# Twelve gate projections as six seven-product pairs in a stage of their own, with input sums made during attention

## The chip, the cores and the metric

The kernel runs on one core of one Trainium2 chip. The metric is device time in microseconds (us) from the start to the end of one launch. Engines are named as the profile names them: PE is the matrix engine (PEld its weight loads), DVE the vector engine, ACT the scalar engine, POOL the GpSimd engine, and SP the engine whose queue issues most DMAs. PSUM is the matrix engine's accumulation memory, of which a bank holds a 128x512 float32 tile. Each engine works through its instructions in the order in which they were written.

## The reference

One decoder layer on x of 1024 tokens by 1024 features, all in float32:

```python
mod = silu(c) @ w_ada + b_ada                     # six rows of 1024: shift_m .. gate_f
u = x * (1 + scale_m) + shift_m
qa, ka, va, qb, kb, vb, ga, gb = split(u @ w_in)  # ga, gb: 1024 columns each
ya = window_attention(qa, ka, va) @ w_branch_a
yb = dilated_attention(qb, kb, vb) @ w_branch_b   # three patterns, merged
y = (sigmoid(ga) * ya + sigmoid(gb) * yb) @ w_o
x = layer_norm(ALPHA * x + (1 + gate_m) * y)
u = x * (1 + scale_f) + shift_f
h = u @ w_gate_up; y = (silu(h_g) * h_u) @ w_down
out = layer_norm(ALPHA * x + (1 + gate_f) * y)
```

The change concerns the sixteen 128-column chunks of `ga` and `gb` (numbers 0 to 15 here), the gates.

## The kernel before

Every float32 product is made of three fp32r matmuls. Both operands are split into a high part (an ACT copy to fp32r) and a low part (a DVE subtraction), and `mac` adds high by high, high by low and low by high (lines 138 to 140). A matmul takes 128 rows of weights by 512 tokens. The tokens stand in two halves t = 0 and 1, the 1024 features in eight blocks k.

`Weights` (object `ws`) is the list of weight pieces of 128x512 in the order of their use. `ws.step` takes the next one: the DMA into `w_raw` (three buffers, sent ahead on SP's queue), the ACT copy to `w_hi` and the DVE subtraction to `w_lo` (lines 78 and 79, four buffers). Where a piece has a scale (the pieces of w_o and w_down), POOL multiplies the raw piece first (line 62).

The stages that matter here, with their times in the profile:

- Attention, to 785 us. Projections of u, scores, exponentials and weighting are interleaved. Gates 3, 6, 4 and 5 are made here too, and their sigmoids stored in `ga_d` in memory. The attention outputs go to memory (`oa_d`, `ob_d`).
- Gates and branches, 785 to 1053.6 us. There are 24 branch steps (`steps`, b = 0, 1, 2 by eight chunks dc), each of 24 matmuls of an attention output (`o_hl`, split by `o_part`) with a chunk of branch weights, and `merge` puts the result into `zt`: for b = 0 an ACT copy, for b = 1 a DVE addition and a POOL multiplication by the gate, for b = 2 a DVE multiplication by the gate into `gy` and a POOL addition (line 968). A list `order`, worked out ahead, puts one gate projection (`make_gate`, 48 matmuls of u with two weight pieces) in front of each branch step that needs one. Twelve gates are made here. `split_merged` then splits the merged chunks into `m` (lines 118 and 119).
- Between these, `ada_steps` is a generator that makes the rows 2 to 5 of `mod`: for each row m, eight DMAs of `a_raw`, one DVE multiplication and seven DVE multiply-adds into `acc` (lines 915 and 917), and at the end of the row a short PE matmul of `acc` with ones (line 926 or 933). One `next(ada)` does one of about ten steps of a row, and 41 of them finish all four. They are called from `make_gate` (twice in each of ten gates) and after each branch step.
- The product with w_o, from 1053.6 us, which opens with eight PSUM banks, one for each block of 128 tokens.
- The feed-forward stage, 1144 to 1569 us. It treats two output chunks with the two token halves and the two feature halves as a 2x2 block product and needs seven half products in place of eight (`PRODUCTS`). Each half product is 12 matmuls. Sums of weight pieces are made by POOL (`g_sums`, four additions for a pair), and sums of the input (`t1` to `t4`) by DVE.

Of the kernel before, what the change touches and what calls it, by code (L numbers as in the profile page):

```python
# [10 lines left out]
F32 = mybir.dt.float32  # L11
# [85 lines left out]

@with_exitstack
def decoder_layer(ctx: ExitStack, tc: tile.TileContext, I, out, dbg=None):
# [28 lines left out]
    def wide(name, pool, halves=(0, 1)):  # L128

        ts = {(s, t, k): pool.tile([P, 4, TH], F32R, name=f"{name}{s}{t}{k}", tag="big")  # L130
              for t in halves for k in range(2) for s in range(2)}
        return lambda s, t, k: ts[s, t, k // 4][:, k % 4]

    u = wide("u", bigu)
# [22 lines left out]
    gate_of = {8 + dc: 46 + dc for dc in range(KC)}  # L157
    gate_of.update({16 + dc: 54 + dc for dc in range(KC)})
    branch_w = [I["w_branch_a"][0], I["w_branch_a"][1], I["w_branch_b"]]
    made_early = [8 + dc for dc in (early_gate_dc, lead_gate_dc, *tail_gates)]  # L160
    bridge = 10
    order = []
    for i in range(len(steps)):
        g = 8 if i == 0 else i + 1
        if g in gate_of and i != 7:
            order.append(("g", g))
        if i == 0:
            order.append(("b", bridge))
        order.append(("w", i))
    for kind, i in order:  # L170
        if kind == "b" or (kind == "g" and i not in (*made_early, bridge)):
            add_chunk(I["w_in"][gate_of[i]], 2, 4)
        elif kind == "w":
            b, dc = steps[i]
            add_chunk(branch_w[b][dc], 1, 4)
# [41 lines left out]
    ga_d = dram.tile([KC, P, T], F32, name="ga_d")  # L217
# [9 lines left out]
    with tc.tile_pool(name="pro", bufs=2) as pro:  # L227
# [55 lines left out]
        def ada_sum(j, ss=(0, 1)):  # L283
# [4 lines left out]
            if j not in mod_t:  # L288
                mod_t[j] = pro.tile([P, 2], F32, name="mod", bufs=3)
# [385 lines left out]
    def send_sums(p):  # L675
# [5 lines left out]
        side(p)[0].dma_start(wa_d[p].rearrange("h (b q) -> (h b) q", q=P), sr[:16])  # L681

    def fetch_bcast(key, src):
        last = key == A_PAIRS - 1 or key in [(B_PAIRS - 1, g) for g in range(3)]
        wb = att.tile([P, T], F32, name="vt" if last else "wb", bufs=1)
        for h in range(2):
            side(key)[0].dma_start(wb[h * 64:(h + 1) * 64], src[h:h + 1].to_broadcast([64, T]))
        sums[key] = wb

    def side(p):  # L690

        return (nc.gpsimd, nc.gpsimd) if p == A_PAIRS - 1 else (nc.sync, nc.vector)

    def scale_a(p):
        o = outs.pop(p)
        side(p)[1].tensor_tensor(o, o, sums.pop(p), op=OP.mult)
        side(p)[0].dma_start(oa_d[p], o)
# [819 lines left out]
```

## Time and profile before

| what | value |
|---|---|
| runs | 1816.66, 1817.24, 1817.37 us, median 1817.24 |
| the profiled execution | 1817.83 us, of which the span from first to last instruction is 1816.1 us |
| busy time: PE, DVE, ACT, POOL | 1802.8, 1071.2, 763.0, 572.6 us |
| stage of gates and branches | 785.1 to 1053.6 us, 268.5 us |

The span leaves out 1.7 us that lie around it. A row of the timeline gives the start in us, the busy time in us, engine, line, operation, the names and shapes of what it writes and reads, how many were merged into the row, and in brackets the idle time ahead of it and what ended that. Matmuls overlap, so the busy time of one is longer than the distance between two.

### The profile page before, as it was taken

What the parts mean: (1) busy time and instruction counts of PE and PEld (TensorE: products, weight loads), DVE (VectorE), ACT (ScalarE), POOL (GpSimd) and SP (SyncE); (2) the same over time, 40 slices, a digit from 0 to 9 for tenths busy, and PEclk for the clock granted to TensorE, in tenths of its full rate; (3) what the DMA queues carried; (4) which work ended last, traced back from release to release, by engine and by line L of the source; (5) the groups of instructions that cost most, each with busy time, mean ns of one, the idle gap of its engine ahead of it and who ended that gap; (6) DMA issues with size and microseconds to landing.
All of it is one profiled execution on the core that took longest, in us unless ns stands there. A gap on an engine that the chain in (4) does not pass through costs nothing.

```text
span 1816.1 us, 24384 instructions
## 1 busy us (share of the span) xinstructions
PE 1802.8 (99%) x8978; PEld 1484.6 (82%) x8978; DVE 1071.2 (59%) x1979; ACT 763.0 (42%) x1650; POOL 572.6 (32%) x372
## 2 busy tenths in 40 slices
PE   9999999999999999999999999999999999999998
PEld 7888888888888888788888888788888888888886
DVE  7754466556556766533654466766565444764557
ACT  6644444444444777643121133743333333421122
POOL 0232233233333232110421253156574333532223
PEclk9999999999999999999999999999999999999999
DMA  9322232232231232254633223042222222442222
GB/s 360 93 74 69 54 89 83 60 88 82 60 83 65 68 99 70 82 181 168 232 122 134 104 99 128 12 151 82 84 79 82 93 82 88 151 141 79 93 76 93
DMA packets 78008, 187.60 MB, mean 103 GB/s; under 512 B 14081, under 2 KB 15681, under 8 KB 77889
## 3 DMA queue, kind: packets, MB, share of 16 engines
q1 hardware_dynamic: 77408, 184.92, 31.1%
q8 instruction: 71, 1.16, 0.3%
q0 software_dynamic: 336, 1.06, 0.2%
q14 instruction: 49, 0.39, 0.1%
q10 hardware_dynamic: 144, 0.07, 0.0%
HBM read 147.37 MB, written 25.00 MB: 95 GB/s over the span
## 4 chain that ended last, share of the span: by engine, by line
PE 89%; DVE 5%; ACT 2%; issue 1%; DMA 1%; POOL 1%; SPq 0%; DVEq 0%
PE pf L1222 22%; PE pj L138 8%; PE pj L140 8%; PE pj L139 8%; PE p L138 6%; PE p L140 6%; PE p L139 6%; PE pf L140 5%; PE pf L138 5%; PE pf L139 5%; PE s L583 4%; PE po L644 3%; PE pt L621 3%; DVE qs L525 1%; DMA wa<-in_w_ada_m 1%
## 5 line engine op out<-in xcount | busy, mean ns | idle before, releaser
L138 PE MATMUL pj<-u,w_hi 128*128 128x512 f32 x736 | 302.8, 411 | 0.0
L140 PE MATMUL pj<-u,w_lo 128*128 128x512 f32 x736 | 288.5, 392 | 0.0
L139 PE MATMUL pj<-u,w_hi 128*128 128x512 f32 x736 | 288.1, 391 | 0.0
L510 POOL TENSOR_TENSOR rb<-rb,sin_t 128x512 f32<-128x512 f32 x64 | 85.7, 1339 | 517.2 <-DVE rb L508 452.3
L119 DVE TENSOR_TENSOR w_lo<-r,w_hi 128x512 fp32r<-128x512 f32 x106 | 114.4, 1082 | 132.9 <-ACT w_hi L118 132.9
L79 DVE TENSOR_TENSOR w_lo<-w_raw,w_hi 128x512 fp32r<-128x512 f32 x148 | 132.9, 902 | 90.5 <-ACT w_hi L78 88.7
L138 PEld LDWEIGHTS pj<-u,w_hi 128*128 128x128 f32 x736 | 138.7, 188 | 31.4 <-issue 6.7
L140 PEld LDWEIGHTS pj<-u,w_lo 128*128 128x128 f32 x736 | 138.3, 188 | 30.7
L599 ACT ACTIVATE probs<-probs,st 128x128 f32<-128x128 f32 (+1 forms) x320 | 145.6, 461 | 32.6 <-DVE st L588 32.3
L139 PEld LDWEIGHTS pj<-u,w_hi 128*128 128x128 f32 x736 | 138.9, 189 | 22.2
L140 PE MATMUL pf<-wd,h 128*128 128x512 f32 x352 | 137.1, 389 | 0.0
L139 PE MATMUL pf<-wd,h 128*128 128x512 f32 x352 | 137.1, 389 | 0.0
L138 PE MATMUL pf<-wd,h 128*128 128x512 f32 x352 | 137.1, 389 | 0.0
L62 POOL TENSOR_TENSOR w_raw<-w_raw,gate 128x512 f32<-128x512 f32 x60 | 84.9, 1432 | 151.0 <-DMA w_raw<-in_w_down 124.7
L1430 DVE SCALAR_TENSOR_TENSOR zt<-zt,pf 128x512 f32<-128x512 f32 x112 | 75.3, 685 | 80.1 <-PE pf L140 80.1
L511 POOL TENSOR_TENSOR r<-ra,rb 128x512 f32<-128x512 f32 x63 | 115.4, 1832 | 4.9
L78 ACT ACTIVATE w_hi<-w_raw 128x512 fp32r<-128x512 f32 x148 | 90.7, 623 | 40.8 <-PE p L139 28.1
L623 ACT ACTIVATE ptsb<-pt 128x512 f32<-128x512 f32 (+1 forms) x128 | 63.5, 549 | 101.5 <-PE pt L621 101.3
L583 PE MATMUL s<-kh,qs 128*128 128x256 f32 (+1 forms) x320 | 79.7, 283 | 2.1 <-DVE st L588 1.5
L524 ACT ACTIVATE qs<-r 64x1024 fp32r<-64x1024 f32 x38 | 40.2, 1058 | 98.7 <-POOL r L511 98.2
L525 DVE TENSOR_TENSOR qs<-r,qs 64x1024 fp32r<-64x1024 f32 x38 | 46.3, 1219 | 57.3 <-ACT qs L524 56.6
L583 PE MATMUL s<-kl,qs 128*128 128x256 f32 (+1 forms) x320 | 80.0, 279 | 0.0
(323 smaller groups left out, 4279.7 us busy)
## 6 DMA issues: line engine op xcount, KB each, us to landing
w_raw<-in_w_in SPq DMA_DIRECT2D x116, 256.0 KB
r<-in_w_gate_up SPq DMA_DIRECT2D x44, 512.0 KB
a_raw<-in_w_ada SPq DMA_DIRECT2D x32, 512.0 KB
w_raw<-in_w_down SPq DMA_DIRECT2D x44, 256.0 KB
h_raw<-h_d SPq DMA_DIRECT2D x22, 512.0 KB
h_d<-g SPq DMA_DIRECT2D x39, 256.0 KB
wa<-in_w_ada_m SPq DMA_DIRECT2D x16, 512.0 KB
kh<-kh SPq DMA_DIRECT2D x26, 256.0 KB
```

Source lines behind the costliest of these rows:

```text
L62: self.nc.gpsimd.tensor_tensor(self.raws[i], self.raws[i], scale(), op=OP.mult)
L78: self.nc.scalar.activation(hi, raw, AF.Copy)
L79: self.nc.vector.tensor_tensor(lo, raw, hi, op=OP.subtract)
L119: nc.vector.tensor_tensor(lo, src, hi, op=OP.subtract)
L138: nc.tensor.matmul(ps, w[0], m[0], start=first, stop=False)
L139: nc.tensor.matmul(ps, w[0], m[1], start=False, stop=False)
L140: nc.tensor.matmul(ps, w[1], m[0], start=False, stop=last)
L510: eng.tensor_tensor(b, b, sin_t[:, s], op=OP.mult)
L511: eng.tensor_tensor(residue_half(res, r, t), by_residue(a, r), by_residue(b, r), op=OP.add)
L583: nc.tensor.matmul(pss[h][:, i, lo:], box["q"][h][:, b * P:(b + 1) * P], ks[h][:, (b - 1 + lo) * P:(b + 1) * P], start=i == 0 and n == 0, ...
L599: nc.scalar.activation(pr, pr, AF.Exp, scale=-1.0, bias=st[:, 0, h, b:b + 1], accum_out=st[:, 1, h, b:b + 1])
L1222: nc.tensor.matmul(ps, w[:, c], m[:, k], start=first and k == 0 and n == 0, stop=k == 3 and n == 2, skip_group_check=True)
```

## The change

The seven-product form is taken over for the twelve gates that were made among the branches. They become six pairs (`gate_pairs`), made in a stage of their own between attention and the branches. The functions of the feed-forward stage for weight sums and splits move into a class `Pairs`, which both stages use. POOL makes the weight sums of the gates as well.

The sums of the input are made while attention runs (`input_sums`, eight times): two DMAs bring parts of x back into the buffer `cst`, two ACT instructions make u of them, four DVE subtractions the sums, and one DMA stores them in `t_d`. The new stage loads them again, 16 tiles `xs` of 128x512, and splits each (`next_sums`).

The first eight half products (two for each of the first four pairs) need the parts of u alone and open the stage. In them pieces of `ws` serve as weights. All sixteen gates now go through `ga_d`, and each branch step of b = 1 and 2 loads its gate (`fetch_gate`). The branch steps follow each other without gates between them. The steps of `ada_steps` are called 14 times in the new stage and 24 times after the branch steps, and the rest is run off behind the last `split_merged`, as before in the code.

The scaling of the last attention pair moves from POOL to DVE, into `o_part`; `split_merged` takes one chunk after each of the last six branch steps, and the chunks 6 and 7 at the end.

```diff
+class Pairs:
...
+    def add(self, p, step, own=None):
+        r1, r2 = self.raws[p]
+        tt = self.nc.gpsimd.tensor_tensor
+        if step == 0:
+            self.sums[p] = own or [self.pool.tile([P, TH], F32, name=n, bufs=1) for n in ("s1", "s2")]
+            tt(self.sums[p][0], r2[:, H0], r2[:, H1], op=OP.add)
+        elif step == 1:
+            tt(self.sums[p][1], self.sums[p][0], r1[:, H0], op=OP.subtract)
+        elif step == 2:
+            tt(r2[:, H0], r1[:, H0], r2[:, H0], op=OP.subtract)
+        else:
+            tt(r1[:, H1], r1[:, H1], self.sums[p][1], op=OP.subtract)
...
+    gate_pairs = ((0, 1), (2, 7), (8, 9), (10, 11), (12, 13), (14, 15))
+    EARLY_PAIRS = 4
+    for x, _ in gate_pairs[:EARLY_PAIRS]:
+        add_chunk(I["w_in"][46 + x], 2, 4)
+    for b, dc in steps:
+        add_chunk(branch_w[b][dc], 1, 4)
...
+        if n % 3 and n < 12:
+            input_sums(*divmod(2 * (n // 3) + n % 3 - 1, 2), i)
...
+        if i == 1:
+            for h in range(2):
+                part, mod = buf[:, h * TH:(h + 1) * TH], mods[k + 4 * h]
+                nc.scalar.activation(part, part, AF.Identity, bias=mod[:, 0:1], scale=mod[:, 1:2])
+        elif i == 2:
+            nc.vector.tensor_tensor(r11, r12, r11, op=OP.subtract)
+            nc.vector.tensor_tensor(r12, r22, r12, op=OP.subtract)
+            nc.vector.tensor_tensor(r22, r22, r11, op=OP.subtract)
+            nc.vector.tensor_tensor(r21, r21, r22, op=OP.subtract)
...
+    for n in range(2 * EARLY_PAIRS):
+        p, i = divmod(n, 2)
+        acc.setdefault(p, []).append(ps_2.tile([P, TH], F32, name="p2"))
+        product(gw, acc[p][i], i, True)
+        while len(gw.ready) < min(3, 2 * EARLY_PAIRS - 1 - n):
+            piece()
+        prepare(n + 4 - 2 * EARLY_PAIRS)
+        next_sums(2)
+        after()
...
+            prepare(n + 3)
...
+            product(gw, ps[bank], i, i in (0, 1, 3))
...
+            if i in (2, 3, 4) and not last:
+                gw.add(p + 1, i - 2)
+            if i == 4 and p + 2 < len(gate_pairs):
+                gw.load(p + 2)
...
+            elif p and i in (1, 2, 4, 6) or (p == 1 and i == 3):
                 next(ada, None)
...
-    for kind, i in order:
-        if kind == "b":
-            make_gate(i, kept=True, then=lambda: parts.append(o_part(0)))
-            continue
-        if kind == "g":
...
+    for i, (b, dc) in enumerate(steps):
...
         for t in range(2):
             merge(b, dc, t, ps[t], gts.get(i))
         next(ada, None)
-        if i == 22:
-            split_merged(range(3, 6))
+        fetch_gate(i + 1)
+        if i == 2 * KC + 1:
+            mg, _ = wide("m", bigu)
+        if i >= 2 * KC + 2:
+            split_merged((i - 2 * KC - 2,))
     split_merged(range(6, 8))
     for _ in ada:
         pass
```

Two places show how the order on the engines moves. The first is the passage from the last branch step to the product with w_o. On PE, the matmuls of `acc` with ones that finish row 5 stood inside a gate projection before (`u` with `w_hi` and `w_lo`):

```order
L140 MATMUL p_9296<-u_82,w_lo 128x512
L926 MATMUL p_9324<-acc,ones 128x512
L926 MATMUL p_9327<-acc,ones 128x512
L138 MATMUL p_9296<-u_82,w_hi 128x512
L139 MATMUL p_9296<-u_83,w_hi 128x512
```

Now they stand between the last matmul of the last branch step (`o_hl`) and the first of the product with w_o (`m`):

```order
L193 MATMUL p_9700<-o_hl,w_lo 128x512
L998 MATMUL p_9761<-acc,ones 128x512
L998 MATMUL p_9764<-acc,ones 128x512
L191 MATMUL p_9770<-w_hi,m_9452 128x512
L192 MATMUL p_9770<-w_lo,m_9452 128x512
```

So the matmuls of row 5 now stand at the seam of the two stages; before they stood 80 rows of PE ahead of it.

On DVE, before, the last branch step was followed by its two gate multiplications (`gy`) and the four splits of chunks 6 and 7:

```order
L79 TENSOR_TENSOR w_lo<-w_raw,w_hi 128x512 x2
L967 TENSOR_TENSOR gy<-p_9444,gt 128x512
L967 TENSOR_TENSOR gy<-p_9445,gt 128x512
L119 TENSOR_TENSOR m_9374<-zt,m_9373 128x512
L119 TENSOR_TENSOR m_9378<-zt,m_9377 128x512
L79 TENSOR_TENSOR w_lo<-w_raw,w_hi 128x512 x5
```

Now the last two multiply-adds of row 5 (`acc`) are there too. The first follows the gate multiplications, ahead of the two splits of chunk 5:

```order
L1196 TENSOR_TENSOR gy<-p_9699,gt 128x512
L1196 TENSOR_TENSOR gy<-p_9700,gt 128x512
L989 SCALAR_TENSOR_TENSOR acc<-a_raw,c_act,acc 128x1024
L170 TENSOR_TENSOR m_9455<-zt,m_9454 128x512
L170 TENSOR_TENSOR m_9459<-zt,m_9458 128x512
```

Four more splits, of chunks 6 and 7, follow these two. The last two of them and what comes behind (`gate` is row 5, finished from what the PE matmuls of `acc` give):

```order
L170 TENSOR_TENSOR m_9455<-zt,m_9454 128x512
L170 TENSOR_TENSOR m_9459<-zt,m_9458 128x512
L989 SCALAR_TENSOR_TENSOR acc<-a_raw,c_act,acc 128x1024
L999 TENSOR_TENSOR gate_9759<-p_9761,gate_9759 128x512
L999 TENSOR_TENSOR gate_9759<-p_9764,gate_9759 128x512
```

The last multiply-add stands behind all of these splits, and the PE matmuls of `acc` read what it writes.

The second place is the start of the new stage, on ACT. Before, the weights of gate 0 were followed by the attention outputs and by the tanh of a gate:

```order
L759 ACTIVATE r<-pj 128x512
L78 ACTIVATE w_hi<-w_raw 128x512 x2
L118 ACTIVATE o_hl<-o_raw 128x1024 x3
L759 ACTIVATE gt<-p_7599 128x512
L759 ACTIVATE gt<-p_7600 128x512
L78 ACTIVATE w_hi<-w_raw 128x512
```

Now weight pieces alternate with the loaded sums `xs`, two by two:

```order
L825 DMA ga_d<-r 128x1024
L78 ACTIVATE w_hi<-w_raw 128x512 x2
L1019 ACTIVATE t2h<-xs 128x512 x2
L78 ACTIVATE w_hi<-w_raw 128x512
L1019 ACTIVATE t2h<-xs 128x512 x2
L78 ACTIVATE w_hi<-w_raw 128x512
L1019 ACTIVATE t1h<-xs 128x512 x2
```

Each `w_hi` of an opening product, from the third piece made here on, stands behind copies that wait for a load from memory.

More of the change, by code (lines that the diff above doesn't have):

```diff
@@ L939, in decoder_layer @@
     gts = {}
[L941 to L956 removed]
+    B = {}
@@ new lines, in next_sums, with piece @@
+    def next_sums(n):
+        for _ in range(n):
+            if t_todo:
+                name, k = t_todo.pop(0)
+                split_to(name, k, t_raw.pop((name, k)))
+                if len(t_todo) > 3:
+                    load_sum(*t_todo[3])
+    def piece():
+        ws.step()
+        gw.ready.append(ws.done[ws.used][:2])
+        ws.used += 1
+    gw.load(0)
+    for x in t_todo[:4]:
+        load_sum(*x)
+    gw.load(1)
+    for step in range(4):
+        gw.add(0, step)
+    acc, gated = {}, {}
@@ L958, in merge, with mrg, fetch_gate @@
+    after()
+    after()
+    gp_ctx.close()
+    zp = ctx.enter_context(tc.tile_pool(name="zp", bufs=2, side="right", reuse_waits="tile"))
+    merged = [zp.tile([P, 4, T], F32, name="zt", tag="zt") for _ in range(2)]
+    def mrg(dc, t):
+        return merged[dc // 4][:, dc % 4, t * TH:(t + 1) * TH]
+    def fetch_gate(i):
+        if KC <= i < len(steps):
+            gts[i] = mix.tile([P, T], F32, name="gt", bufs=2)
+            nc.sync.dma_start(gts[i], ga_d[i - KC])
     def merge(b, dc, t, ps, g):
@@ L1010, in decoder_layer @@
             ws.step()
+        if (b == 0 and 2 <= dc < 6) or (b == 1 and dc in (3, 5)):
+            following.append(o_part(low))
+        if b == 1 and dc == KC - 1:
+            following += [o_part(low) for _ in range(2)]
+        if dc == KC - 1:
+            parts, following = following, []
         for t in range(2):
@@ L1209, in g_split @@
-    def g_split(p, i):
-        hi, lo = [wpool.tile([P, 512], F32R, name=s, tag=s, bufs=4) for s in ("w_hi", "w_lo")]
-        split(hi, lo, g_source(p, i))
-        ready.append((hi, lo))
-    def product(ps, i, first, between=None):
-        hi, lo = ready.pop(0)
-        b = B[PRODUCTS[i]]
-        for k in range(4):
-            if k == 3 and between:
-                between()
-            c = slice(k * P, (k + 1) * P)
-            for n, (w, m) in enumerate(((hi, b[0]), (hi, b[1]), (lo, b[0]))):
-                nc.tensor.matmul(ps, w[:, c], m[:, k], start=first and k == 0 and n == 0, stop=k == 3 and n == 2,
-                                 skip_group_check=True)
@@ L1291, in decoder_layer @@
         if n:
-            g_split(*opening[n + 3])
+            gu.split(*opening[n + 3])
         if n in (2, 4, 6):
```

342 lines of the change are left out of this document (204 added, 138 removed).

## The prediction

> **What bounds the kernel now.** I read the page's busy times first, then who makes PE wait, then windows over the stages, then the timeline at the seam that the change rebuilds. The first row gives busy time, share of the span and count; the second is the largest wait of PE for another engine (total us, times, longest).
>
> ```profile
> PE 1802.8 (99%) x8978; PEld 1484.6 (82%) x8978; DVE 1071.2 (59%) x1979; ACT 763.0 (42%) x1650; POOL 572.6 (32%) x372
> PE s L583 <- DVE st L588: 1.5, 6, 0.3
> ```
>
> PE is busy for 1802.8 of 1816.1 us, and its largest wait adds up to 1.5 us. So the kernel lasts as long as PE has work, and fewer matmuls shorten it, as long as nobody makes PE wait. The next rows are windows (length, then busy us and count of PE, PEld, DVE, ACT, POOL, then granted clock, DMA share, GB/s): attention, the stage of gates and branches, the opening of the seven-product form in the feed-forward stage, one pair of that form later on, and the load at the start of the kernel.
>
> ```profile
> 58.40:785.00 726.60, 724.54 (x4180) 594.67 (x4178) 435.01 (x1132) 386.24 (x1038) 207.81 (x130) 1.00 0.27 77
> 785.10:1053.60 268.50, 268.50 (x1194) 221.56 (x1195) 138.17 (x167) 69.49 (x116) 56.50 (x38) 1.00 0.45 156
> 1163.40:1182.40 19.00, 18.08 (x77) 14.02 (x76) 18.56 (x29) 16.42 (x29) 1.60 (x1) 1.00 0.07 23
> 1278.00:1297.00 19.00, 19.00 (x86) 15.74 (x85) 11.14 (x11) 7.26 (x14) 12.27 (x7) 1.00 0.23 83
> 15.00:20.00 5.00, 3.86 (x16) 2.58 (x15) 3.93 (x7) 3.86 (x5) 0.00 (x0) 1.00 1.03 413
> ```
>
> Gates and branches leave PE no gap at all, with DVE half idle. The form that is now copied holds PE at 19.00 of 19 us in its steady state, but lost 0.92 us in its opening, where DVE was busy for 18.56 of 19 us.
>
> **The matmuls taken away.** Twelve gates of 48 matmuls are 576; six pairs of 84 are 504. So 72 of 128x512 fall away. Their price is not the 0.39 us of a row but the distance between two:
>
> ```profile
> 1042.67 0.39 PE L138 MATMUL p<-o_hl,w_hi 128*128 128x512 f32 x1
> ...
> 1053.33 0.39 PE L140 MATMUL p<-o_hl,w_lo 128*128 128x512 f32 x1
> 1053.56 0.39 PE L138 MATMUL p<-w_hi,m 128*128 128x512 f32 x1
> ```
>
> The first of these rows opens the last but one branch step and the third follows the last, so 48 matmuls take 10.89 us, 0.227 us each. **Term 1: 72 x 0.227 = -16.3 us.** By the 0.39 us it would be -28, which overlapping work does not give.
>
> **The input sums in attention.** Eight times two ACT copies with scale, four DVE subtractions of 128x256, two loads and one store. By the split of a 128x512 tile (0.69 us alone, below), half of it for a subtraction: 32 x 0.35 = 11 us of DVE; 16 x 0.62 us = 10 us of ACT. In attention DVE idles for 292 us and ACT for 340. Behind these on their engines stand the reductions and exponentials of scores, for which PE waits. The loads stand on SP behind weight pieces, and `cst` is shared with the softmax merge, whose DMAs are a unit (some 40 us) away. **Term 2: 0**, with an upper end of 2 us, if each of the eight makes PE wait once for the 0.3 us of the wait row, and a lower end of 0, as none is removed. The last pair's scaling (POOL before, DVE in `o_part` now) is under the cover of branch matmuls both times.
>
> **The opening and the pairs.** Eight products of 12 x 0.227 = 2.72 us, 21.8 us. DVE has in them 9 low parts of weights and 16 of `xs`, 25 x 0.62 = 15.5 us, and three additions and sigmoid steps, 4 us: 19.5 of 21.8. The copied form lost 0.92 us at such a load. The loads run in two sets of two buffers: 1.2 us to issue, about 3 us to land (the row below is a 512 KB store from POOL's queue; none of SP's is timed), two ACT copies 1.24 and a split 0.62 make 6.1 us, so a set per 3.0 us against 2.72 of PE.
>
> ```profile
> oa_d<-o POOLq DMA_DIRECT2D x1, 512.0 KB, 3.0
> ```
>
> Then the first four pairs have five products left, 13.6 us, with five POOL instructions and three or four `ada` steps each. DVE's own part is 5 x 0.62 + 4 x 1.28 + 0.69 + 3 x 0.4 = 10.1 us, and POOL holds it up (below) by up to 5 x 1.05 = 5.3 us: 15.4 against 13.6 at the worst, with two products (5.4 us) of lead. **Term 3: +1.5 us**, near the measured 0.92, with ends 0 (the steady pair's row) and 8 (four pairs by 1.8 us and 1 us of opening). Gates stored and loaded add some 17 MB to a stage of 252 us, 67 GB/s on top of 156; the start moved 413 GB/s, so I cost that at nothing.
>
> **The seam, where I expect the gain to go.** Behind the last branch step PE now has the matmul of `acc` that finishes row 5, ahead of all of w_o. It needs the last multiply-add, which DVE has behind two gate multiplications, another multiply-add and six splits. `next(ada)` is called 14 + 24 = 38 times where 41 are needed; before there were 20 + 24 = 44, and row 5 was done 80 PE rows earlier. This seam before, on DVE and POOL:
>
> ```profile
> 1044.03 3.70 DVE L119 TENSOR_TENSOR m<-zt,m 128x512 fp32r<-128x512 f32 x6
> 1047.64 0.69 DVE L79 TENSOR_TENSOR w_lo<-w_raw,w_hi 128x512 fp32r<-128x512 f32 x1
> 1054.96 1.28 DVE L79 TENSOR_TENSOR w_lo<-w_raw,w_hi 128x512 fp32r<-128x512 f32 x2
> 1056.16 1.28 DVE L967 TENSOR_TENSOR gy<-p,gt 128x512 f32<-128x512 f32 x2
> 1057.36 6.57 DVE L119 TENSOR_TENSOR m<-zt,m 128x512 fp32r<-128x512 f32 x4
> 1056.99 2.99 POOL L968 TENSOR_TENSOR zt<-zt,gy 128x512 f32<-128x512 f32 x2 [4.91 <-DVE gy L967]
> 1059.95 5.13 POOL L62 TENSOR_TENSOR w_raw<-w_raw,gate 128x512 f32<-128x512 f32 x3
> L917 DVE SCALAR_TENSOR_TENSOR acc<-a_raw,c_act,acc x28: 1272/1279/2234, 819.8 to 1021.8; 128x1024 f32<-128x1024 f32 x28
> ```
>
> Six splits alone took 3.70 us, 0.62 each. Four of them beside POOL's additions and scalings took 6.57 in place of 2.5: each of the four POOL instructions that ran meanwhile cost DVE about 1.05 us. The two take turns on what they read, which a single pair shows too: the POOL addition grew from 1.3 to 2.26 us behind a multiply-add, and the split after it from 0.69 to 1.78.
>
> ```profile
> 998.26 1.27 DVE L917 SCALAR_TENSOR_TENSOR acc<-a_raw,c_act,acc 128x1024 f32<-128x1024 f32 x1
> 998.42 2.26 POOL L968 TENSOR_TENSOR zt<-zt,gy 128x512 f32<-128x512 f32 x1 [1.43 <-DVE gy L967]
> 999.45 1.78 DVE L79 TENSOR_TENSOR w_lo<-w_raw,w_hi 128x512 fp32r<-128x512 f32 x1
> ```
>
> Before, the last branch matmul ended at 1053.33 + 0.39 = 1053.72 and the last split at 1063.93, 10.2 us later, and PE needed none of it yet. Now two multiply-adds (2.56) and two splits (1.24) are added to this queue, and a fifth POOL instruction falls into it (1.05): 10.2 + 3.8 + 1.0 = 15.0 us until PE may go on. **Term 4: +15.0 us.** Its lower end is DVE without POOL: 2.44 us to the gate multiplications (1056.16), then 1.28 + 1.28 + 6 x 0.62 + 1.28 = 10.0. The row with POOL in it is the nearer one.
>
> DVE may also arrive late. In the last six branch steps it has 0.62 + 1.28 + 1.28 + 1.24 = 4.4 us and two POOL turns of 1.05, 6.5 against 5.44 us of PE, and four POOL scalings beside: 6 x 1.1 + 4.2 = 10.8 us at most, of which the 2.4 us that it waits at the seam anyway and an idle start take their part. PE does not feel this within the steps, since eight banks and three weight pieces of lead cover some 16 us. **Term 5: +1.0 us** (ends 0 and 7), near the lower end because the traced steps show no such lag.
>
> **The restart.** After a stop of this length PE may come back slowly. The nearest row is the kernel's own start, 128x128 matmuls of one line:
>
> ```profile
> 1.06 3.54 PE L275 MATMUL po<-ones 128*128 128x128 f32 x16 [1.06 <-DVE ones L115]
> 6.15 4.85 PE L275 MATMUL po<-ones 128*128 128x128 f32 x42
> 0.00:5.00 5.00, 3.94 (x18) 3.70 (x19) 2.08 (x7) 1.49 (x2) 0.20 (x4) 1.00 0.49 119
> ```
>
> 16 took 0.221 us each and 42 later ones 0.115, so the first 3.5 us cost 1.7 us more than warm ones, though the granted clock reads 1.00 in that window. **Term 6: +1.7 us**, with ends 0 (the clock column) and 1.7. [...]
>
> **The sum.** -16.3 + 0 + 1.5 + 15.0 + 1.0 + 1.7 = +2.9 us on the profiled execution's 1817.83, 1820.7. The median of the runs, 1817.24, is 0.6 below that execution, so I put 1820.1 us: the matmuls are saved and PE waits the time away at the seam.
>
> **The rivals.**
> - The gain mostly arrives. POOL's scalings of w_o come earlier or later than DVE's queue at the seam, the stop is the 10.0 us of the lower end, and terms 3 and 5 are nothing: 1817.24 - 16.3 + 10.0 + 1.7 = 1812.6. For it speak the splits at 0.62 us before 1049; against it that the two POOL additions must lie in this queue, since chunk 7 waits for them.
> - DVE carries its lag to the seam, the opposite side: the six last branch steps need more DVE and POOL time than PE gives them, and the stop grows from 15 to 21 us: -16.3 + 1.5 + 21 + 1.7 = +7.9, 1825.1. It decides where the two POOL turns per step cost more than 1.0 us together. For it speaks 6.5 against 5.44; against it that no traced step lasts so short with these splits.
> - The loads of `xs` set the pace of the opening. If they land in 4.5 us in place of 3, a set takes 3.8 us, and eight sets exceed their products by 8 x 1.1 = 8.6 us, since the weight copies stand behind them on ACT: +2.9 - 1.5 + 8.6 = +10, 1827.2. Above about 3.5 us of landing it decides. The first 3 MB of loads are issued together there, which speaks for it.
> - That the change takes nothing from PE I exclude: its queue holds exactly 72 matmuls fewer.
>
> **How the numbers follow.** The forecast gets 0.42, the arriving gain 0.27, the carried lag 0.16, the loads 0.15. A change of 0.2%, 3.6 us, is about what a measurement of this kernel can tell from none. The forecast's own spread is 1816 to 1823, two thirds of it within 3.6 us of the median (0.27 same, 0.15 slower). The arriving gain gives 0.22 faster and 0.05 same, the carried lag 0.16 slower, the loads 0.11 slower and 0.04 same. Together 0.22 faster, 0.36 same, 0.42 slower. All lower ends give 1817.24 - 16.3 + 10.0 = 1810.9, all upper ends 1817.24 - 16.3 + 2 + 8 + 15 + 7 + 1.7 = 1834.6. The range 1811 to 1828 leaves out the sum of several upper ends.
>
> **What the changed profile would show.** PE waits for DVE `acc` (line 989) once, for 10 to 20 us, at about 1037 us, and the stage of gates and branches then lasts about 255 us of PE work and that wait. If this row is short or missing, terms 4 and 5 are wrong and the kernel is faster. `xs` waits on ACT and PE waits for `w_lo` of line 145 between 785 and 830 would prove the third rival, a PE wait above 17 us the second. The pace of the first matmuls after the stop tells term 6, PE waits in attention term 2. The prediction is wrong above all if PE does not stand at that one matmul.

## The result and the profile after

The changed kernel takes 1837.54 us (median of 4 runs, 1836.59 to 1841.31) against 1817.05 us before: ratio 1.0117, 95% interval 1.0099 to 1.0134. It is slower by 20.5 us, where 2.9 us were forecast and the range ended at 1828. The profiled execution took 1837.64 us, with a span of 1835.9 us, 19.8 us more than before.

The busy time of PE and its largest waits (total us, times, longest), from the page and the view of waits of the changed kernel:

```profile
PE 1794.7 (98%) x8906; PEld 1472.8 (80%) x8906; DVE 1144.2 (62%) x2056; ACT 811.2 (44%) x1726; POOL 619.3 (34%) x397
...
PE p L998 <- DVE acc L989: 18.7, 1, 18.7
PE s L624 <- DVE qs L566: 4.9, 4, 1.5
PE p L1030 <- DVE w_lo L79: 2.1, 1, 2.1
...
PE p L1030 <- ACT gt L1125: 1.7, 1, 1.7
```

PE has 8906 instructions, 72 fewer than before: the matmuls are gone. But it waits in three places: at the seam for `acc`, in attention for the queries `qs`, and in the opening of the gate stage. The forecast had a price for the first and the last, and none for attention. Windows over these (length, busy us and count of PE, PEld, DVE, ACT, POOL, then granted clock, DMA share, GB/s): attention, the opening, the branch steps, the wait at the seam, and what follows it.

```profile
58.40:785.00 726.60, 720.03 (x4120) 590.36 (x4119) 446.58 (x1159) 393.07 (x1039) 207.41 (x129) 1.00 0.30 87
...
793.20:834.40 41.20, 37.11 (x157) 28.89 (x158) 30.07 (x42) 24.49 (x44) 12.63 (x8) 1.00 0.79 275
...
900.00:1050.12 150.12, 150.12 (x678) 124.51 (x677) 105.33 (x108) 48.77 (x77) 54.85 (x33) 1.00 0.63 213
1050.12:1068.80 18.68, 0.00 (x0) 0.00 (x0) 18.63 (x17) 4.08 (x7) 12.65 (x8) 0.56 0.63 211
1068.80:1072.60 3.80, 3.80 (x5) 1.74 (x6) 0.69 (x1) 0.00 (x0) 0.00 (x0) 0.50 0.00 0
```

In the first row PE did 60 instructions fewer in the same 726.6 us than before (x4120 against x4180). In the fourth it does nothing for 18.68 us while DVE is busy for 18.63; in the fifth its clock is granted at half.

Where the 19.6 us between the last matmuls of the two executions come from (starts of single matmuls in the two timelines; the first gate matmul starts at 785.10 before and 793.18 after, the last of the branches at 1053.33 and 1049.73, the first of w_o at 1053.56 and 1071.59, the last of all at 1807.83 and 1827.47):

| stretch | before | after | difference |
|---|---|---|---|
| to the first gate matmul | 785.1 | 793.2 | +8.1 |
| gates and branches | 268.2 | 256.6 | -11.7 |
| seam, to the first matmul of w_o | 0.2 | 21.9 | +21.6 |
| from there to the last matmul | 754.3 | 755.9 | +1.6 |

Row 5's four matmuls, 1.7 us at the normal pace with the slower matmul behind them, moved from the second stretch to the third. So gates and branches lost 6.3 us of what they should have saved (16.3 + 1.7 less 11.7).

### The profile page after: what moved, and what is told of

Same layout as the page of the kernel before. It is cut to its first block, busy times and chain, and to the rows that moved or that the text cites. A ratio compares the mean times of both kernels' runs of the same rounds, so it can differ in the third digit from the quotient of the medians.

```text
span 1835.9 us, 24586 instructions
## 1 busy us (share of the span) xinstructions
PE 1794.7 (98%) x8906; PEld 1472.8 (80%) x8906; DVE 1144.2 (62%) x2056; ACT 811.2 (44%) x1726; POOL 619.3 (34%) x397
## 4 chain that ended last, share of the span: by engine, by line
PE 85%; DVE 7%; ACT 3%; issue 2%; DMA 2%; POOL 1%; SPq 0%; DVEq 0%; POOLq 0%
PE pf L1030 22%; PE pj L191 8%; PE pj L193 8%; PE pj L192 8%; PE pf L191 5%; PE pf L193 5%; PE pf L192 5%; PE p L1030 4%; PE s L624 4%; PE p L191 3%; PE p L193 3%; PE p L192 3%; PE pt L662 2%; PE po L685 2%; DVE qs L566 1%
## 5 line engine op out<-in xcount | busy, mean ns | idle before, releaser
L145 DVE TENSOR_TENSOR w_lo<-r,w_hi 128x512 fp32r<-128x512 f32 x128 | 135.1, 1058 | 137.6 <-ACT w_hi L144 137.2
L79 DVE TENSOR_TENSOR w_lo<-w_raw,w_hi 128x512 fp32r<-128x512 f32 x132 | 120.9, 919 | 85.0 <-ACT w_hi L78 84.4
L78 ACT ACTIVATE w_hi<-w_raw 128x512 fp32r<-128x512 f32 x132 | 81.8, 622 | 104.5 <-PE p L192 47.3
L126 POOL TENSOR_TENSOR s<-r 128x512 f32<-128x512 f32 x27 | 35.6, 1320 | 173.2 <-DVE w_lo L145 98.5
```

The lines of the kernel that those rows point to most:

```text
L78: self.nc.scalar.activation(hi, raw, AF.Copy)
L79: self.nc.vector.tensor_tensor(lo, raw, hi, op=OP.subtract)
L145: self.nc.vector.tensor_tensor(lo, src, hi, op=OP.subtract)
```

## The experiments

| run | what it is | median us | ratio to before, 95% interval |
|---|---|---|---|
| changed kernel | | 1837.5 | 1.0099 to 1.0134 |
| e2_no_subs_4_7_10 | 12 of 32 subtractions left out | 1831.3 | 1.0068 to 1.0093 |
| e9_before_plus_sums | before, with the input sums | 1825.1 | 1.0030 to 1.0055 |
| e6_subs_on_pool | those 12 on POOL | 1832.9 | 1.0074 to 1.0101 |
| e10_subs_on_pool_early | on POOL, a quarter unit earlier | 1831.4 | 1.0061 to 1.0087 |
| e3_before_row5_late | before, row 5 at the seam | 1834.7 | 1.0081 to 1.0112 |
| e1_row5_early | row 5 ahead of the seam | 1824.9 | 1.0031 to 1.0058 |
| e5_row5_spread | the same, spread | 1821.9 | 1.0019 to 1.0039 |
| e15, e16 | seam filled, too long; shorter | 1850.2; 1836.3 | 1.0165 to 1.0192; 1.0084 to 1.0118 |
| e4_sums_start_later | opening, splits later | 1837.6 | 1.0098 to 1.0126 |
| e7_loads_in_order | opening, loads reordered | 1835.3 | 1.0085 to 1.0112 |
| e11_loads_five | opening, five tiles | 1839.4 | 1.0105 to 1.0136 |
| e14_sums_loaded_once | 12 of 16 loads left out | 1834.1 | 1.0079 to 1.0106 |
| e8_three_mended | spread, POOL, loads in order | 1817.2 | 0.9989 to 1.0007 |
| e12_all_mended_2 | other places, five tiles | 1813.5 | 0.9967 to 0.9986 |
| e13_all_mended_3 | those places, loads of e7 | 1809.9 | 0.9944 to 0.9971 |

### The sums in attention

Here the forecast had nothing, and 8.1 us went. The timeline before, at the scores of a new pair of heads: `ra` opens the rotation of the queries, which goes over POOL and ACT and ends in the two splits `qs` on DVE; PE then makes the scores `s`.

```profile
286.03 0.68 DVE L507 TENSOR_TENSOR ra<-pj,cos_t 128x512 f32<-128x512 f32 x1
...
293.96 1.22 DVE L525 TENSOR_TENSOR qs<-r,qs 64x1024 fp32r<-64x1024 f32 x1
...
294.90 0.28 PE L583 MATMUL s<-kl,qs 128*128 128x128 f32 x1
...
295.24 0.19 PEld L583 LDWEIGHTS s<-kh,qs 128*128 128x128 f32 x1 [0.20 <-DVE qs L525]
```

The split ends at 295.18, the matmul that needs it starts at 295.24 with its weight load, which had already waited 0.20 us for it. This chain had no slack before the change. After, the same place:

```profile
283.67 2.05 DVE L777 TENSOR_TENSOR o<-o 128x1024 f32<-128x1024 f32 x1
...
285.62 0.43 DVE L883 TENSOR_TENSOR cst<-cst 128x256 f32<-128x256 f32 x1
...
287.00 0.42 DVE L886 TENSOR_TENSOR cst<-cst 128x256 f32<-128x256 f32 x1
...
287.34 0.68 DVE L548 TENSOR_TENSOR ra<-pj,cos_t 128x512 f32<-128x512 f32 x1
...
295.20 1.22 DVE L566 TENSOR_TENSOR qs<-r,qs 64x1024 fp32r<-64x1024 f32 x1
...
296.47 0.33 PE L624 MATMUL s<-kh,qs 128*128 128x128 f32 x1 [1.54 <-DVE qs L566]
```

Four subtractions of the input sums (285.62 to 287.34) stand directly ahead of `ra`, 1.7 us; ten us later PE stops for 1.54. This comes three times (near 296, 431 and 563 us); before, the same three splits ended 0.05 to 0.06 us ahead of their matmuls. The other five sums stand in units without the scaling of attention outputs (`o<-o`), and no stop of this size follows them. Four of them stand ahead of chains that had over 2 us of slack before: one split ended at 162.42 us and its matmul started at 164.54.

Three stops of 1.54 us are 4.6 of the 8.1 us. Behind two of them PE's granted clock is at half for 3.4 us, which costs some 1.6 us each (worked out in the last section), and that is most of the rest.

The first test leaves out the subtractions in the three places:

```diff
+        elif i == 2 and c == 0 and k:
+            pass
         elif i == 2:
```

> Leaves out the four subtractions of the input sums on DVE in three of the eight places (the first column half of k = 1, 2, 3), so that t_d is not the sums there; loads, ACT copies and stores stay. Theory: in these three places the 1.7 us of subtractions stand directly ahead of the rotation (ra, rb) whose chain over POOL, ACT and DVE ends at the scores of the next pair, with about 0.2 us to spare; they cause the three stops of 1.54 us, and two of the stops start a stretch of half-pace matmuls that costs about 1.7 us each: 3 x 1.54 + 2 x 1.7 = 8.0, so 1829.5 us, and attention ends at about 785 us. Rival: the loads, stores and ACT copies (12.9 us of ACT) make the delay, and attention stays within 1.5 us of 793: 1836 to 1837.5 us.

Measured: 1831.3 us, 6.2 less, and the first gate matmul starts at 785.68 in place of 793.18, 7.5 less. Loads, ACT copies and stores stayed, so the rival falls. The waits of PE:

```profile
PE p L1000 <- DVE acc L991: 18.8, 1, 18.8
...
PE s L624 <- DVE qs L566: 0.4, 1, 0.4
```

The three stops are gone, the seam is as it was. The opposite test puts only the sums into the kernel before: `input_sums` as it stands in the change, its call, the tile `mods` that keeps the scales for it, and `t_d`, which nothing reads.

```diff
+        if n % 3 and n < 12:
+            input_sums(*divmod(2 * (n // 3) + n % 3 - 1, 2), i)
```

> The kernel before with the input sums alone: loads, ACT copies, subtractions and stores of t_d in attention as in the changed kernel, and nothing reads t_d. Theory: the sums by themselves bring the three stops of 1.54 us in the later places of the first column half and, in two of three, a stretch of 3.4 us at half pace: 3 x 1.5 + 2 x 1.7 = +8 us at most, +4.6 without a half-pace stretch: 1821.6 to 1825.1 us. Rival: the stops in attention come from another part of the change (the moved order of the first gate pieces, the last pair's scaling moved to DVE), and the time stays within 1 us of 1817.0.

Measured: 1825.1 us, 7.8 more than the 1817.4 of the kernel before beside it. The first gate matmul starts at 793.07, and the wait that had been 0.4 us in all is

```profile
PE s L585 <- DVE qs L527: 4.6, 3, 1.5
```

So the term that was zero in the forecast is 8 us by itself, with the rest of the change absent. Two ways to move the 12 subtractions were tried. First, on POOL at the same place:

```diff
         elif i == 2:
-            nc.vector.tensor_tensor(r11, r12, r11, op=OP.subtract)
+            eng = nc.gpsimd if c == 0 and k else nc.vector
+            eng.tensor_tensor(r11, r12, r11, op=OP.subtract)
...
```

> The four subtractions of the input sums run on POOL in place of DVE in the three places where PE stopped; nothing is left out. Theory: DVE's queue ahead of the rotation is what stops PE, and POOL has 6.8 us idle there, so attention ends at 785 to 786 us as where the subtractions were left out: 1829.5 to 1831.5 us. Rival: POOL is in the same chain (rb, r) and takes turns with DVE on their reads; its four instructions (about 0.7 us each) push DVE's own o<-o by 2 us or POOL's rb, and the stops stay: 1835 to 1838 us.

Measured: 1832.9 us, between the two. Three stops of 1.0 us stay:

```profile
PE s L624 <- DVE qs L566: 3.5, 4, 1.0
```

DVE scales `o<-o` at the same time and takes 2.46 us for it in place of 2.05, and POOL's subtractions take up to 2.42 us where one alone takes 0.74. The two engines hold each other up, so a part of the 1.7 us comes back to DVE. One quarter of a unit earlier, right behind the ACT copies, POOL is idle and the queries' rotation is still to come:

```diff
-        elif i == 2:
+        if i == (1 if c == 0 and k else 2):
+            eng = nc.gpsimd if c == 0 and k else nc.vector
...
```

> As in the run with the subtractions on POOL, but one quarter of a unit earlier, right behind the ACT copies, where DVE does not scale the attention outputs of the pair ahead of the rotation of the queries. Theory: the stops of 1.0 us that stayed there came from POOL and DVE taking turns while DVE scaled (o<-o); away from it they go, attention ends at 785 to 786 us and the time is 1829.5 to 1831 us. Rival: POOL's subtractions wait there for the ACT copies with POOL's rotation (rb, r) behind them, and new stops appear: 1832 to 1837 us.

Measured: 1831.4 us (1828.9 to 1832.3), 0.4 above the expected end. In the timeline of POOL the subtractions now lie well ahead of the rotation (`rb`):

```profile
270.79 0.73 POOL L884 TENSOR_TENSOR cst<-cst 128x256 f32<-128x256 f32 x1 [11.76 <-ACT cst L881]
...
274.60 0.74 POOL L887 TENSOR_TENSOR cst<-cst 128x256 f32<-128x256 f32 x1
278.38 1.29 POOL L551 TENSOR_TENSOR rb<-rb,sin_t 128x512 f32<-128x512 f32 x1 [3.05 <-DVE rb L549]
```

PE no longer waits for `qs`, and the first gate matmul starts at 784.50. With nothing left out, attention is as long as before the change.

### The seam

The changed kernel's timeline, with the gate multiplications of the last three branch steps first (the last step's last matmul ends at 1050.12):

```profile
1041.44 1.29 DVE L1196 TENSOR_TENSOR gy<-p,gt 128x512 f32<-128x512 f32 x2
...
1049.66 1.27 DVE L1196 TENSOR_TENSOR gy<-p,gt 128x512 f32<-128x512 f32 x2
...
1056.58 1.27 DVE L1196 TENSOR_TENSOR gy<-p,gt 128x512 f32<-128x512 f32 x2
...
1057.78 1.90 DVE L989 SCALAR_TENSOR_TENSOR acc<-a_raw,c_act,acc 128x1024 f32<-128x1024 f32 x1
...
1059.60 7.95 DVE L170 TENSOR_TENSOR m<-zt,m 128x512 fp32r<-128x512 f32 x6
1060.76 5.04 POOL L62 TENSOR_TENSOR w_raw<-w_raw,gate 128x512 f32<-128x512 f32 x3
...
1067.47 1.27 DVE L989 SCALAR_TENSOR_TENSOR acc<-a_raw,c_act,acc 128x1024 f32<-128x1024 f32 x1
...
1068.80 3.78 PE L998 MATMUL p<-acc,ones 128*128 128x512 f32 x4 [18.68 <-DVE acc L989]
...
1071.59 1.34 PE L191 MATMUL p<-w_hi,m 128*128 128x512 f32 x1
```

The queue is the one that was foretold: six splits take 7.95 us beside POOL, where six alone took 3.70 before, four turns of 1.06. From the gate multiplications to the end of the last multiply-add are 12.2 us (12.6 by the forecast's sum: 15.0 less the 2.44 to the multiplications). What is longer is its start: 6.5 us behind the last matmul in place of 2.4, because DVE carries a lag out of the last branch steps. PE makes a step in 5.44 us, but the gate multiplications of the last three start 8.2 and 6.9 us apart, so that they come 2.2, 5.0 and 6.5 us behind their steps' last matmuls.

Is it this one matmul alone? The kernel before with only the first six steps of the mod rows passed over among the gates:

```diff
+    skip_ada = [0] * 6
...
-                next(ada, None)
+                skip_ada.pop() if skip_ada else next(ada, None)
```

> The kernel before, with the first six steps of the mod rows among the gates left to the end, so that row 5's matmul stands at the seam as in the changed kernel; nothing else of the change. Theory: DVE's queue there is two gate multiplications, a multiply-add, four splits and a multiply-add, with POOL's additions and three scalings: 2.4 + 1.3 + 1.3 + 2.5 + 1.3 + 5 x 1.05 = 14.0 us, less 0.4 to the end of the matmul, and 2.0 us of slow matmuls behind it: 1817.1 + 13.6 + 2.0 = 1832.7 us. Rival: the seam is only late in the changed kernel, because splits and multiply-adds of six branch steps push DVE there; the stop here is then below 5 us and the time under 1823.

Measured: 1834.7 us, 17.6 more. The placement of six small steps costs that without any other part of the change:

```profile
PE p L926 <- DVE acc L917: 15.1, 1, 15.1
```

The other way round, six more steps in the changed kernel, after the first six branch steps:

```diff
         next(ada, None)
+        if i < 6:
+            next(ada, None)
         fetch_gate(i + 1)
```

> Six more steps of the mod rows after the first six branch steps (two each there), so that row 5's matmul on PE stands after branch step 20 and no longer at the seam. Theory: the matmul of acc at the seam costs the changed kernel its wait of 18.7 us, 2.0 us of half-pace matmuls behind it, and nothing of this comes back elsewhere, while row 5's four warm matmuls (1.9 us) are needed either way; so 1837.5 - 18.7 - 2.0 = 1816.8 us, and the wait for acc is below 1 us. Rival: DVE and POOL are late at the seam whatever PE waits for (gate multiplications 6.5 us after the last branch matmul, the last split 17.3 us after it), so that PE stops for the first w_lo or for a split of the w_o product instead, for 8 to 15 us: 1825 to 1832 us.

Measured: 1824.9 us, 12.6 less, not 20.7. The wait for row 5 is gone, but the placement costs in its turn:

```profile
PE p L1005 <- DVE acc L989: 2.8, 1, 2.8
...
PE p L191 <- DVE gy L1196: 1.7, 1, 1.7
```

Two steps behind one branch step mean that a multiply-add waits for a load that was sent just ahead of it, so row 3 was 2.8 us late for its matmul, with a stretch of matmuls at half pace behind that. A second placement avoids this:

```diff
                 if i >= 4:
                     ws.step()
+                if i < 6:
+                    next(ada, None)
...
         next(ada, None)
+        if i in (4, 13):
+            next(ada, None)
```

> Six more steps of the mod rows in the last gate pair, one behind each of its first six products, and two more after the branch steps 4 and 13, so that row 5's matmul stands after branch step 18, every last multiply-add lies two or more products ahead of its matmul, and no two steps of one row meet where the matmul follows. Theory: what the earlier run with doubled steps lost again was its own placement (2.85 us of waiting for the multiply-adds of row 3 and the half-pace matmuls behind that, 1.75 us at the seam because DVE was still late), so that now 1837.5 - 18.7 - 2.0 = 1816.8 us comes out, 1814 to 1819. Rival: with the stop at the seam gone PE runs into DVE's backlog elsewhere in the branch steps or in the w_o product whatever the placement, and 1822 to 1827 us stays.

Measured: 1821.9 us, 15.7 less: the rival's lower end, so there is a backlog elsewhere. It is in the last gate pair, where the six steps now stand on DVE ahead of the weights' low parts:

```profile
PE p L1030 <- DVE w_lo L145: 3.3, 2, 2.2
```

How much is the wait and how much the slow clock behind it? PE was given work that nothing reads, ahead of row 5's matmul:

```diff
+                    for _ in range(156 if m == 5 and t == 0 else 0):
+                        nc.tensor.matmul(ps[:, :P], ones, ones, start=True, stop=True)
```

> The changed kernel with 156 matmuls of ones by ones (128x128, 0.115 us each) on PE between the last branch step and row 5's matmul, 17.9 us of work that nothing reads, so that PE waits only about 0.8 us for acc in place of 18.7. Theory: the end of the wait is set by DVE and stays; what goes is the slow restart, with the granted clock at 0.50 for 3.4 us, which cost 2.0 us: 1835.5 us, 1834.5 to 1836. Rival: the restart costs nothing at the seam, since what is behind waits for DVE's splits anyway: 1837 to 1838 us. Against both: were the filling longer than the wait, the time would be above 1838.5.

Measured: 1850.2 us. In the trace each of these matmuls is two instructions, 0.112 us apart, so the filling took 34.8 us and overran the wait; the run says nothing on the question. With half as many (against the run above):

```diff
-                    for _ in range(156 if m == 5 and t == 0 else 0):
+                    for _ in range(78 if m == 5 and t == 0 else 0):
```

> The filled seam with half as many matmuls: 78 of ones by ones are 156 passes of 0.112 us, 17.5 us, so that PE waits about 1.3 us for acc in place of 18.7. Theory: the end of the wait is DVE's and stays, the slow restart goes: its four matmuls of acc 1.5 us faster and what follows in the w_o product 1.1 us, 1837.5 - 2.6 = 1834.9 us, 1834 to 1836. Rival: nothing is gained, 1837 to 1838 us.

```profile
1051.29 17.58 PE L999 MATMUL p<-ones 128*128 128x128 f32 x156
1070.69 1.98 PE L1000 MATMUL p<-acc,ones 128*128 128x512 f32 x4 [1.81 <-DVE acc L989]
1072.11 0.79 PE L191 MATMUL p<-w_hi,m 128*128 128x512 f32 x1
```

Measured: 1836.3 us (1834.3 to 1837.4), 1.2 less; the intervals overlap. In the traces row 5's matmuls take 1.4 us to the first of w_o, where they took 2.8 behind the full stop, and that one takes 0.63 to the next in place of 1.18. So by the traces the slow restart is 2.0 us of the loss, which the times can't confirm by themselves, and the wait is the rest.

### The opening of the gate stage

In the window from 793.20 to 834.40 above PE has 157 matmuls, 35.6 us at 0.227, so 5.6 of the 6.3 us lie in it. The first stop and the second:

```profile
802.47 1.32 ACT L1019 ACTIVATE t2h<-xs 128x512 fp32r<-128x512 f32 x2 [6.50 <-DMA xs<-t_d]
803.13 2.39 DVE L1020 TENSOR_TENSOR t2l<-xs,t2h 128x512 fp32r<-128x512 f32 x2 [6.37 <-ACT t2h L1019]
...
804.94 1.70 POOL L130 TENSOR_TENSOR r<-r,r 128x512 f32<-128x512 f32 x1
805.45 1.74 DVE L79 TENSOR_TENSOR w_lo<-w_raw,w_hi 128x512 fp32r<-128x512 f32 x1
...
807.25 0.51 PE L1030 MATMUL p<-u,w_lo 128*128 128x512 f32 x1 [2.15 <-DVE w_lo L79]
...
825.55 0.50 PE L1030 MATMUL p<-t3h,w_hi 128*128 128x512 f32 x1 [1.66 <-ACT gt L1125]
```

ACT stands idle 6.5 us for the first sum, with the next weight piece behind it; DVE's splits are stretched by POOL's additions (2.39 us for the two of `t2l`, where two of `t1l` took 1.29 at 811.11 with POOL idle); PE stops. That is the third rival's picture, with 3.8 us of stops where it had 8.6. The DMA engines have no time to spare there (DMA share 1.02, 386 GB/s):

```profile
800.00:809.00 9.00, 6.82 (x30) 4.98 (x29) 5.87 (x5) 2.83 (x5) 6.31 (x4) 1.00 1.02 386
```

Four edits tried to part the causes. First, the splits of the sums from the third product on:

```diff
-        next_sums(2)
+        next_sums(2 if n >= 2 else 0)
```

> The splits of the loaded input sums start behind the third opening product, not the first, so that the weights' copies and splits of the first pieces no longer stand behind them on ACT and DVE. Theory: the stop of 2.15 us for w_lo goes, and the later one of 1.66 us (bank held by an ACT copy) stays or grows by up to 1 us: 1837.5 - 2.2 = 1835.4, at best 1834.5. Rival: POOL's four additions, which stretch DVE's splits by 1.05 us each in the same 6.4 us, make the stop; then it stays within 1 us wherever the splits stand, 1836.5 to 1838.5 us, or the late sums make a longer stop.

Measured: 1837.6 us, no change. The weight piece is now ahead of the sums on ACT, but it is late itself. Its DMA (line 55 of SP, three issues) and the copy that waited for it:

```profile
800.68 2.17 SPq L55 DMA_DIRECT2D w_raw<-in_w_in  x3
...
809.35 0.63 ACT L78 ACTIVATE w_hi<-w_raw 128x512 fp32r<-128x512 f32 x1 [12.63 <-DMA w_raw<-in_w_in]
```

8.7 us from issue to use, behind the loads of two pairs (2 MB) and of four sums (1 MB). So the loads were put in order:

```diff
     gw.load(0)
-    for x in t_todo[:4]:
-        load_sum(*x)
-    gw.load(1)
...
+        if n == 0:
+            for x in t_todo[:4]:
+                load_sum(*x)
+        if n >= 2:
+            next_sums(2)
+        if n == 4:
+            gw.load(1)
```

> In the opening of the gate stage the loads of pair 1 (1 MB) are sent behind the fifth product and those of the first four input sums behind the first, the sums' splits start behind the third: the opening weight pieces are no longer behind 3 MB of other loads. Theory: the stop of PE in the opening is the weight piece that lands 8.7 us after its issue, with the memory at about 400 GB/s and 3 to 4 MB sent ahead of it; with these behind it the stop of 2.2 to 2.9 us goes and 1 us at most stays for the late sums: 1837.5 - 3 = 1834.5 us, 1833.5 to 1835.5. Rival: the total traffic of this stretch, not its order, sets the pace; the stop moves to the input sums or to pair 1's weights and the time stays at 1836.5 to 1838.5.

Measured: 1835.3 us, as expected in size, but not as expected in the trace: the first stop is gone, and the second grew from 1.7 to 3.4 us. The stage lasts 256.7 us as without the edit (256.6), but in this execution 6.8 of them, from 821.1 on, at half the clock. The same with five tiles, begun earlier:

```diff
-        t_raw[name, k] = gp.tile([P, TH], F32, name="xs", bufs=4)
+        t_raw[name, k] = gp.tile([P, TH], F32, name="xs", bufs=5)
...
-        if n >= 2:
+        if n >= 1:
             next_sums(2)
-        if n == 4:
+        if n == 5:
             gw.load(1)
```

> The opening's loads in order, as in the run before with that edit, but with five tiles for the input sums in place of four and their splits from the second product on; pair 1's load behind the sixth. Theory: what was left of the opening's loss (3.4 us of waiting for a bank that an ACT copy held, since ACT waited for one input sum after the other) is the time from a sum's split to the next one's landing; a fifth tile and an earlier start shorten it to 0 to 2 us: 1833 to 1835.5 us. Rival: the memory gives what it gives, about 400 GB/s, and the stop only changes place: 1835 to 1838 us.

Measured: 1839.4 us, 4 more than with four tiles. Last, 12 of the 16 loads of sums left out:

```diff
-                split_to(name, k, t_raw.pop((name, k)))
-                if len(t_todo) > 3:
-                    load_sum(*t_todo[3])
+                split_to(name, k, t_raw["t2", k])
```

> The changed kernel with 12 of the 16 loads of input sums left out: the four tiles loaded first serve for all 16 splits, so t1, t3 and t4 hold the values of t2; ACT's and DVE's work is the same. Theory (loads pace the opening): the later stop of 1.66 us, and the small ones, go, and 3 MB less traffic lets the weight pieces land earlier, so that the first one of 2.15 us shrinks too: 2 to 4.4 us less, 1833 to 1835.5 us. Rival (ACT and DVE work, and POOL's turns, pace it): the stops of 2.2 and 1.7 us stay where they are, 1836.5 to 1838 us.

Measured: 1834.1 us. The second stop is gone without these loads, the first stays:

```profile
PE p L1030 <- DVE w_lo L79: 2.2, 1, 2.2
```

So the second stop comes from the loads of the later sums, and the first does not need them. How much of the time each is worth stays open: kernels with the same code in this stage as the changed one lasted 255.6 to 257.9 us in it in their single profiled executions, and e4 (257.4), e7 (256.7) and e14 (256.3) lie inside that. The clock hides a part of it. In e14 it read 0.50 for 6.8 us from the first stop on, while in the changed kernel's opening it read 1.00 throughout:

```profile
804.13:810.95 6.82, 6.16 (x15) 4.79 (x16) 6.82 (x10) 4.62 (x9) 1.74 (x2) 0.50 0.46 136
```

At 1.6 us for 3.4 us of half clock, e7 and e14 lost an estimated 3.2 us by it in these executions, so the length of the stage says little of either edit.

### The edits together

The edits of e5 (mod rows), e6 (POOL) and e7 (loads):

> The three edits together: mod rows spread, subtractions of the three places on POOL, loads in order. Theory, if the losses are separate and add up: 1837.5 - 20.7 - 7 - 3 = 1806.8 us, that is 16.3 us of matmuls less 6 us that stay (1817.1 - 16.3 = 1800.8 is what the matmuls alone would give); 1804 to 1811 us, faster than before. Rival: the three stops cover each other (a stop in one place lets DVE and the loads catch up for the next), and the sum falls short by more than 5 us: 1812 us or more.

Measured: 1817.2 us, the same as before the change, so the rival: each edit kept some waits of its own, as seen above. Next, a third placement of the mod rows (the lines below are against e5), the subtractions as in e10, and the loads as in e11:

```diff
-                if i < 6:
+                if i < 3:
                     next(ada, None)
...
-        if i in (4, 13):
+        if i in (5, 6, 7):
             next(ada, None)
```

> Mod rows spread (three more steps in the last gate pair, doubled after the branch steps 5, 6 and 7), subtractions on POOL one quarter earlier, loads with five tiles. Theory: of the 14.6 us of PE waits in the first version with three edits, 3.0 in attention go, 3.9 in the opening shrink to 1.5, and 2.7 in the last gate pairs (DVE with the mod rows) go: 1817.2 - 3 - 2.4 - 2.7 - 1.5 (slow stretches behind them) = 1807.6 us; 1805 to 1811 us, faster than before. Rival: each edit moves DVE's and the memory's work into another wait of the same size, and 1814 to 1818 us stay.

Measured: 1813.5 us, 0.2% faster than before, between theory and rival. The same with the loads of e7 in place of e11's:

> As the second version with three edits, but with the loads in the order that gained 2.3 us by itself (four tiles, pair 1's load behind the fifth product) in place of five tiles, which lost 1.9 us. Theory: 1813.5 - 4.2 = 1809.3 us, 1807.5 to 1811.5. Rival: with attention's stops gone the opening starts at another phase of the loads and loses the same in either order: 1812 to 1815 us.

Measured: 1809.9 us (1809.0 to 1810.8) against 1817.5: ratio 0.9958, 0.9944 to 0.9971, the fastest of all and faster than the kernel before. Its waits:

```profile
PE p L1031 <- ACT gt L1129: 2.7, 1, 2.7
...
PE p L191 <- DVE gy L1202: 1.3, 1, 1.3
...
PE p L1031 <- DVE w_lo L145: 1.1, 1, 1.1
```

Attention ends at 785.33, the stage is 9.9 us shorter than before in place of 16.3, and the rest 1.6 us longer. Most of what is missing in the stage lies in the opening (the 2.7 us and 3.4 us of half clock behind them), some of it in the last pairs (the 1.1 us).

## Why the prediction was wrong

Its terms and what the two traces show for them:

| term | forecast | measured |
|---|---|---|
| 1, matmuls taken away | -16.3 | -16.3 (72 fewer, same pace) |
| 2, input sums in attention | 0 (0 to 2) | +8.1 |
| 3, opening and pairs | +1.5 (0 to 8) | +6.3 |
| 4 and 5, wait at the seam | +16.0 | +18.7 |
| 6, restart | +1.7 | +2.0 |
| not named | 0 | +0.7 |
| sum | +2.9 | +19.5 |

- **Term 2 is the step that failed.** "In attention DVE idles for 292 us" was right and beside the point. The forecast counted the work nearly right (11 us of DVE, measured 14.6; 10 of ACT, 12.9) and named what stands behind it, but priced a possible wait by the 0.3 us of the largest wait row. That row is what was left over with the work of before, and no bound for what an insertion of 1.7 us makes of it. The `qs` rows of before, which were not read, showed 0.06 us of slack in the three units where the stops came and 2 us in others. e2 and e9 show both ways that the subtractions at these three places, or the sums alone, make the loss.
- **Term 3** was inside its ends, but its value was taken from the copied form's opening, which has no such loads. The third rival (loads of `xs` set the pace) is what the waits show, with +6.3 where it had +8.6. The loads of the later sums cause the second stop (e14); the first goes when the loads are reordered (e7) and stays without the later ones. What each is worth in time is not shown.
- **Term 4** had the right place and mechanism, and e3 shows it alone: 15.1 us of wait. **Term 5** was too small: DVE reached the gate multiplications 4.0 us later than before, near the middle of its ends, where 1.0 was taken "because the traced steps show no such lag". Those steps had other work: before, the last multiply-add started at 1021.8 us, and the twelve splits of the chunks 0 to 5 lay in two blocks behind 1044 us; now each of the last six steps holds a split pair and a multiply-add. That was the second rival's mechanism.
- **Term 6** held: half the granted clock from 1068.80 to 1072.6. Row 5's matmuls took 1.5 us longer than before (2.79 to the first of w_o, where they took 1.31 to the next gate matmul), and the one behind them 0.5 us longer (1.18 against 0.64).
- The range reached to 1828 by taking one rival at a time. Three of the terms came out at once on the upper side, and they do not exclude each other.

## What to carry to other kernels

Price an insertion by the slack of the chain that it stands ahead of, read at its own place in the timeline (when does the consumer start, when did the producer end), not by the idle share of its engine or by today's largest wait. A piece of work left to the end of an in-order queue costs all that was queued ahead of it, on the engine that waits in order as well: six missing steps of 1.3 us each cost 17.6 us here. When several such losses are possible in different stages, add them: two of the three, brought into the kernel before one at a time, cost 7.8 and 17.6 us there, and mending all three gave back 27.6 us.

## What the runs showed of the hardware

- A short stop of PE cost twice in some cases here. The same stop of 1.54 us in attention was followed in some by 3.4 us of matmuls at about twice their distance (0.43 us in place of 0.23), and in others by none. Windows of the changed kernel behind the first such stop (which ends at 296.47) and the second (430.94):

```profile
297.89:301.30 3.41, 3.41 (x9) 2.68 (x9) 3.38 (x2) 0.69 (x2) 3.33 (x2) 0.50 0.00 0
...
430.94:436.00 5.06, 5.05 (x28) 4.37 (x29) 5.03 (x5) 2.99 (x10) 3.57 (x2) 1.00 0.11 40
```

  Half the clock and 9 matmuls behind the first, the full clock behind the second. Over the traced executions it came behind 13 of 30 stops of 1.5 us and behind none of six of 1.0 us, and it adds about 1.6 us (the first gate matmul starts at 793.2 us with two such stretches, at 790.0 in e5 with none). Executions of one kernel differ, and their mean granted clock with them (the eight of e5 lie between 1819.9 us, at 0.998, and 1825.2 us, at 0.996), and single executions of kernels with such stops should be compared stage by stage.
- Where a stop of 1.54 us fell in time told whether the slow stretch followed. In each trace the granted clock changed at whole multiples of 3.41 us from each other: in the changed kernel it fell at 297.89 and 564.12 us, 78 multiples apart, and at the seam at 1052.23, 143 further on. Counted from the last such point ahead of a stop of 1.54 us, the 13 stops with half the clock behind them began 0.2 to 1.6 us in; of the other 17 one began 1.55 us in and the rest 1.8 to 3.0. This sorts the stops in attention alone; stops in the opening did not follow it as cleanly.
- At the seam the granted clock fell to 0.50 within the wait, and the matmuls took their normal distance again from 1072.8 on, 4 us after work began. The same column had read 1.00 at the start of the kernel before, where the first 16 matmuls were slow as well (0.221 us each, where 42 later ones took 0.115).
- DVE and POOL took turns in these splits, at 1.06 us per POOL instruction: six splits took 3.70 us alone and 7.95 beside four POOL instructions. What moving work from DVE to POOL was worth went with what DVE did meanwhile: in e6, beside DVE's `o<-o`, the move gave back a third of each stop (1.54 to 1.0), in e10, with DVE on other work, all of it.
